# The first layer's modulation weights through a ring of four buffers instead of two

## The chip, the cores and the metric

The kernel runs on one core of one Trainium2 chip. The metric is the device time of one execution in microseconds (us). The kernel before takes 1497.33 us, the median of 3 runs (1495.65 to 1498.18). A difference of 0.2%, about 3.0 us, is what a measurement of this kernel can tell from no change.

## The reference

Two trunk layers are computed for 512 latent tokens and 128 context tokens that share one set of weights (model width 1024). Before each layer, six modulation vectors (shift, scale and gate, for the mixer and for the MLP) come from a conditioning vector:

```python
def ada_params(cond, w, b):
    m = jax.nn.silu(cond) @ w + b
    return jnp.split(m[..., None, :], 6, axis=-1)

def modulate(x, shift, scale):
    return layer_norm(x) * (1.0 + scale) + shift
```

There are two conditioning vectors, one for each kind of token, so `ada_params` is a product of 2 rows with a 1024 x 6144 matrix `ada_w[layer]`: nearly no arithmetic, but 24 MB of weights per layer. Layer 0's mixer is a pair of RG-LRU scans beside a 2-D Fourier mix, layer 1's is attention; after either comes a squared-ReLU MLP with 4096 hidden channels.

## The kernel before

**Weights.** All matmul weights come as units of 128 x 1024 floats (512 KB) in a fixed plan (`stream_plan`). `fetch` (L242) loads unit after unit into 3 `raw` buffers; `split_unit` splits each into a high half (ACT, L173) and a low half (DVE, L174) in one of 4 `sp` buffers. In names such as `raw_17` or `sp_14` the number is the unit's place in the plan. TensorE (PE) multiplies them in three passes (high x high, high x low, low x high). All matmuls but transposes are recorded at L265.

**The even mixer.** The plan begins with: units 1 to 4 (`in`, RNN input), 5 (`gate`), 6 to 9 (`four`), 10 (`gate`), 11 to 13 (`in`, gate chunks), 14 to 16 (`dft`), 17 (`in`), and from 18 the output projection `out`. Units 14 and 15 make the position DFT: 4 chunks of 12 matmuls, 48 in all, with 512 columns each. After it come the context DFT and the channel DFT (`yb_out`), the last gate chunk, and the output projection.

**Modulation weights of layer 0.** A third of them is used in `start`. The other two thirds (groups 1 and 2) are the work of `ada_gen`: a generator that is advanced once by each call of `next`, so once for each unit that PE takes. Each advance is a *step*: two loads of 512 KB (halves 0 and 1 of one block of 128 rows) and four matmuls on 32 columns of the array each (`ada_mm`), which add into one PSUM bank over 8 steps. In this text the steps are numbered 0 to 15; step 7 ends group 1 and step 15 ends group 2. `fill` keeps two loads outstanding: the load for step s+1 goes into the buffer that step s has just read. The buffers are two of the six `n` buffers (128 x 1024 floats each), the same two each time, since `last=True` takes back the buffer that was given back last:

```python
        def fill():
            nonlocal i
            while i < len(todo) and len(q) < 2:
                w = self.n.get([128, 1024], last=i >= 2)
                self.ada_load(*todo[i], w.t)
```

`acc` is one buffer of 128 x 2 x 1024 floats. It holds the sums of `ada_sum_gen`, which makes layer 1's modulation on DVE from the first layer's MLP on; until then nobody uses it.

**What sets the order.** A scheduler orders each engine's instructions when the kernel is built; each engine then runs its own list strictly in that order. Nearly all loads (L242, L381, L345, L337, L965) stand in one list, SP's: a load that has to wait for its buffer holds up all loads behind it.

Of the kernel before, what the change touches and what calls it, by code (L numbers as in the profile page):

```python
# [126 lines left out]
class Kern:  # L127
# [118 lines left out]
    def next(self, key):  # L246
        self.seen += 1
        self.ada_due += self.ada_rate
        while self.ada_due >= 1.0:
            self.ada_due -= 1.0  # L250
            if next(self.ada, None):
                break
        for _ in range(self.side_steps if self.side is not None else 0):
            next(self.side, None)
        assert self.plan[self.pos] == key, (self.plan[self.pos], key)
        self.pos += 1
        if not self.ready:
            self.pump()
        s = self.ready.pop(0)
        self.pump()  # L260
        return s
# [157 lines left out]
    def ada_gen(self, groups):  # L419

        todo = [(l, g, k, half) for l, g in groups for k in range(8) for half in range(2)]
        q = []
        i = 0

        def fill():
            nonlocal i
            while i < len(todo) and len(q) < 2:
                w = self.n.get([128, 1024], last=i >= 2)
                self.ada_load(*todo[i], w.t)
                q.append(w)  # L430
                i += 1
        fill()
        yield
        bank = fin = None
        for l, g, k, half in todo:
            if k == 0 and half == 0:
                bank = self.psum()
            w = q.pop(0)
            self.ada_mm(bank.t, k, half, w.t)
            w.done()  # L440
            fill()
            if k == 7 and half == 1:
                fin = self.ada_finish(l, g, bank)
                next(fin)
            if half == 1:
                yield
                if k == ADA_FIN and fin is not None:
                    next(fin, None)
                    fin = None
        if fin is not None:  # L450
            next(fin, None)

# [1290 lines left out]
```

## Time and profile before

| | before |
|---|---|
| median of 3 runs | 1497.33 us |
| the profiled execution | 1502.44 us |
| its span, first to last instruction | 1500.3 us |
| PE busy | 1443.6 us (96%) |
| DVE, ACT, POOL busy | 944.5, 618.9, 377.9 us |
| mean granted clock of PE, as a share of 2.4 GHz | 0.987 |

The profile is of one execution, 5.1 us above the median. Its traces show each engine's instructions, what ended the idle time before them, and the clock that PE was granted. Times within it count from the span's start.

### The profile page before, as it was taken

Reading aid. Unit: us, or ns where it says so; the run is one execution under the profiler, and the core shown is the slowest. Engines: PE = TensorE matmul, PEld = TensorE weight load, DVE = VectorE, ACT = ScalarE, POOL = GpSimd, SP = SyncE. Lnnn points to the kernel's source line nnn. Section 1 sums busy time; section 2 is a strip of 40 time slices with the busy share of each in tenths; the row PEclk is TensorE's granted clock in tenths of the full one; section 3 lists DMA queues with packets and bytes.
Section 4 is the critical chain, followed back from the end, with each engine's and each line's share of the span. In section 5 each row is a group of like instructions: output and inputs, shape, how many; then the busy total and the mean of one; then the engine's idle time right before and its main releaser. Section 6 shows DMA issues by size and latency. Waiting matters only on the chain. (4 is left out here: it accounts for less than half of the span.)

```text
span 1500.3 us, 21820 instructions
## 1 busy us (share of the span) xinstructions
PE 1443.6 (96%) x8428; PEld 1245.2 (83%) x8428; DVE 944.5 (63%) x1641; ACT 618.9 (41%) x1081; POOL 377.9 (25%) x395
## 2 busy tenths in 40 slices
PE   6999999999999999999799999999999999999997
PEld 4768677988988998998688888878898888998986
DVE  6656767857757663346645345556967893764865
ACT  4467437421321321335456355655631441431441
POOL 1144203202102202002413222321206633524510
PEclk9999999999999999999999999999999999999999
DMA  9354843445345342220633132330545434334441
GB/s 383 133 182 162 292 145 101 166 141 172 130 162 167 128 148 70 71 99 28 224 110 104 63 114 85 123 135 29 171 144 149 101 118 105 92 119 87 124 176 70
DMA packets 63575, 199.72 MB, mean 133 GB/s; under 512 B 11240, under 2 KB 11624, under 8 KB 63472
## 3 DMA queue, kind: packets, MB, share of 16 engines
q1 hardware_dynamic: 58320, 189.38, 36.5%
q0 software_dynamic: 5152, 8.95, 3.7%
q8 instruction: 66, 1.08, 0.3%
q14 instruction: 37, 0.30, 0.1%
HBM read 181.49 MB, written 16.81 MB: 132 GB/s over the span
## 5 line engine op out<-in xcount | busy, mean ns | idle before, releaser
L265 PE MATMUL bank<-R,sp 128*128 128x384 f32 (+3 forms) x4224 | 644.0, 311 | 13.5 <-POOL R L353 4.0
L265 PEld LDWEIGHTS bank<-R,sp 128*128 128x128 f32 x4224 | 620.9, 189 | 31.8 <-POOL R L353 5.8
L265 PE MATMUL bank<-sp,R 128*128 128x512 f32 x2580 | 614.2, 396 | 12.3 <-DVE sp L174 7.2
L265 PEld LDWEIGHTS bank<-sp,R 128*128 128x128 f32 x2580 | 484.2, 190 | 134.3 <-issue 10.3
L174 DVE TENSOR_TENSOR sp<-raw,sp 128x1024 fp32r<-128x1024 f32 (+2 forms) x177 | 235.8, 1334 | 132.6 <-ACT sp L173 130.8
L173 ACT ACTIVATE sp<-raw 128x1024 fp32r<-128x1024 f32 (+2 forms) x177 | 180.7, 1026 | 282.6 <-PE bank L265 254.6
L546 POOL TENSOR_TENSOR R<-R,n 128x512 f32<-128x512 f32 x30 | 45.5, 1557 | 278.0 <-DVE n L543 278.0
L354 DVE TENSOR_TENSOR R<-n,R 128x640 fp32r<-128x640 f32 (+2 forms) x119 | 106.5, 899 | 12.8 <-POOL R L353 9.7
L485 DVE SCALAR_TENSOR_TENSOR acc<-n,cx,acc 128x1024 f32<-128x1024 f32 x84 | 106.9, 1310 | 9.2 <-DMA n<-in_ada_w_dram 9.2
L1073 ACT ACTIVATE n<-bank,pack 128x384 f32<-128x384 f32 (+1 forms) x80 | 38.7, 525 | 138.5 <-PE bank L265 130.2
L351 ACT ACTIVATE R<-n 128x640 fp32r<-128x640 f32 (+1 forms) x96 | 66.9, 704 | 62.0 <-DVE n L1075 31.2
L567 POOL TENSOR_TENSOR ln<-ln,mhalf 128x1 f32<-128x1 f32 x35 | 22.4, 641 | 241.6 <-DVE ln L566 240.6
L565 ACT ACTIVATE junk<-R,ln 128x1024 bf16<-128x1024 f32 x35 | 40.3, 1150 | 86.1 <-DVE ln L575 60.8
L1075 DVE SCALAR_TENSOR_TENSOR n<-n 128x640 f32<-128x640 f32 x40 | 34.8, 871 | 64.3 <-ACT n L1073 64.2
L543 DVE TENSOR_TENSOR n<-bank,vec 128x512 f32<-128x512 f32 x70 | 47.3, 685 | 31.4 <-PE bank L265 29.3
L1423 POOL TENSOR_SCALAR n<-n,mx 128x384 f32<-128x384 f32 (+1 forms) x80 | 43.3, 544 | 90.6 <-DVE mx L1420 49.9
L265 PE MATMUL bank<-R,R 128*128 128x512 f32 x240 | 62.5, 405 | 0.0
L620 ACT ACTIVATE n<-bank,mod 128x128 f32<-128x128 f32 x120 | 45.4, 456 | 25.7 <-PE bank L613 25.7
L265 PEld LDWEIGHTS bank<-R,R 128*128 128x128 f32 x240 | 44.4, 188 | 11.0
L1437 ACT ACTIVATE n<-bank 128x384 f32<-128x384 f32 (+1 forms) x80 | 32.9, 447 | 49.4 <-PE bank L1433 43.0
L173 ACT ACTIVATE sp<-vec 128x1024 fp32r<-128x1024 f32 x24 | 25.3, 1058 | 57.7 <-PE bank L265 57.5
L1408 DVE CUSTOM_DVE_ANT_0 n<-bank,vec 128x256 f32<-128x256 f32 (+3 forms) x128 | 40.6, 350 | 12.9 <-PE bank L265 8.9
(179 smaller groups left out, 1246.9 us busy)
## 6 DMA issues: line engine op xcount, KB each, us to landing
raw<-in_wts_dram SPq DMA_DIRECT2D x184, 512.0 KB, 3.3
n<-in_ada_w_dram SPq DMA_DIRECT2D x80, 512.0 KB, 4.3
vec<-in_rpb_dram SPq DMA_DIRECT2D x16, 512.0 KB, 4.8
R<-in_ada_dram SPq DMA_DIRECT2D x15, 512.0 KB, 10.0
xsum<-n POOLq DMA_DIRECT2D x30, 256.0 KB, 5.6
vec<-in_vecs_dram SPq DMA_DIRECT2D x13, 512.0 KB, 4.6
vec<-gscr SPq DMA_DIRECT2D x10, 512.0 KB, 4.3
R<-in_x_dram SPq DMA_DIRECT2D x5, 512.0 KB
```

What stands on the lines that cost most here:

```text
L173: self.nc.scalar.activation(s.t[:, 0, :cols], src[:, :cols], AF.Copy)
L174: self.nc.vector.tensor_tensor(out=s.t[:, 1, :cols], in0=src[:, :cols], in1=s.t[:, 0, :cols].bitcast(F32), op=OP.subtract)
L265: self.nc.tensor.matmul(out, lhsT, rhs, start=start, stop=stop)
L351: self.nc.scalar.activation(hi, src, AF.Copy)
L354: (self.nc.vector if lo_eng == "dve" else self.nc.gpsimd).tensor_tensor(out=lo, in0=src, in1=hi.bitcast(F32), op=OP.subtract)
L485: nc.vector.scalar_tensor_tensor(acc.t[:, cond, :], w.t, f[cond], acc.t[:, cond, :], op0=OP.mult, op1=OP.add)
L543: nc.vector.tensor_tensor(out=tmp.t[:, :512], in0=o.t, in1=gates[t // 4].t[:, c], op=OP.mult)
L546: nc.gpsimd.tensor_tensor(out=x[:, t, c], in0=x[:, t, c], in1=tmp.t[:, :512], op=OP.add)
L565: nc.scalar.activation(self.junk, src, AF.Square, bias=m[:, 2:3], accum_out=m[:, 4:5])
L620: nc.scalar.activation(dst, tr.t[:, j * 128:(j + 1) * 128], AF.Identity, bias=sh, scale=sc)
L1408: nc.vector.tensor_tensor_reduce(out=p[h].t[:, c0:c1], in0=o[h].t[:, c0:c1], in1=rpb[j, h].t[:, r0:r0 + c1 - c0], scale=1.0, scalar=-3e38, ...
L1423: nc.gpsimd.tensor_scalar(p.t[:, :n], p.t[:, :n], m[:, 5:6], 1.0, op0=OP.mult, op1=OP.mult)
```

## The change

`ada_gen` takes two `n` buffers and the `acc` buffer at its start, holds them until its last step is done, and uses the four places in turn: steps with an even number use the two `n` buffers, steps with an odd number the two halves of `acc`. Four loads are outstanding instead of two.

```diff
     def ada_gen(self, groups):
 
         todo = [(l, g, k, half) for l, g in groups for k in range(8) for half in range(2)]
+        held = [self.n.get([128, 1024]) for _ in range(2)] + [self.acc.get([128, 2, 1024])]
+        bufs = [held[0].t, held[1].t, held[2].t[:, 0], held[2].t[:, 1]]
         q = []
         i = 0
 
         def fill():
             nonlocal i
-            while i < len(todo) and len(q) < 2:
-                w = self.n.get([128, 1024], last=i >= 2)
-                self.ada_load(*todo[i], w.t)
+            while i < len(todo) and len(q) < 4:
+                w = bufs[i % 4]
+                self.ada_load(*todo[i], w)
                 q.append(w)
                 i += 1
         fill()
...
             w = q.pop(0)
-            self.ada_mm(bank.t, k, half, w.t)
-            w.done()
+            self.ada_mm(bank.t, k, half, w)
             fill()
...
+        for w in held:
+            w.done()
         if fin is not None:
             next(fin, None)
```

The scheduler makes new lists from this. In the rows below, `in_ada_w_dram` marks a load of a step and `cx` a matmul of a step; the bank is the step's PSUM bank. Three places differ where the prediction speaks of them.

SP's list around the position DFT, before. `n_48`, `n_49` are step 9's loads, `n_50`, `n_51` step 10's, `n_52`, `n_53` step 11's; `vec` from `gscr` are the gates of group 1:

```order
L381 DMA n_48_1286<-in_ada_w_dram 128x1024
L381 DMA n_49_1290<-in_ada_w_dram 128x1024
L345 DMA vec_5_1750<-gscr 128x1024
L381 DMA n_50_1351<-in_ada_w_dram 128x1024
L381 DMA n_51_1355<-in_ada_w_dram 128x1024
L345 DMA vec_6_1752<-gscr 128x1024
L242 DMA raw_17_1295<-in_wts_dram 128x1024
L242 DMA raw_18_1360<-in_wts_dram 128x1024
L381 DMA n_52_1417<-in_ada_w_dram 128x1024
L381 DMA n_53_1421<-in_ada_w_dram 128x1024
L242 DMA raw_19_1426<-in_wts_dram 128x1024
```

The same place after the change. The pair in `n_11` and `n_12` is step 10's, the pair in `acc_1` behind it is step 11's, and the next pair is step 12's:

```order
L381 DMA n_11_559<-in_ada_w_dram 128x1024
L381 DMA n_12_560<-in_ada_w_dram 128x1024
L381 DMA acc_1_561<-in_ada_w_dram 128x1024 x2
L345 DMA vec_5_1725<-gscr 128x1024
L345 DMA vec_6_1727<-gscr 128x1024
L242 DMA raw_17_1280<-in_wts_dram 128x1024
L242 DMA raw_18_1343<-in_wts_dram 128x1024
L381 DMA n_11_559<-in_ada_w_dram 128x1024
L381 DMA n_12_560<-in_ada_w_dram 128x1024
L242 DMA raw_19_1407<-in_wts_dram 128x1024
```

Step 11's loads have moved ahead of both gate vectors and two weight units.

PE's list from step 10 into the position DFT, before:

```order
L265 MATMUL bank_67_1283<-n_51_1355,cx_118 32x512 x2
L410 MATMUL bank_72_1430<-ident,n_47_1223 128x128 x4
L265 MATMUL bank_73_1452<-sp_14_1292,R_11_877 128x512 x6
L265 MATMUL bank_73_1452<-sp_15_1357,R_11_877 128x512 x6
L265 MATMUL bank_74_1467<-sp_14_1292,R_11_877 128x512 x5
L265 MATMUL bank_67_1283<-n_52_1417,cx_118 32x512 x2
L265 MATMUL bank_74_1467<-sp_14_1292,R_11_877 128x512
L265 MATMUL bank_74_1467<-sp_15_1357,R_11_877 128x512 x2
L265 MATMUL bank_67_1283<-n_53_1421,cx_118 32x512 x2
L265 MATMUL bank_74_1467<-sp_15_1357,R_11_877 128x512 x4
```

and after the change:

```order
L265 MATMUL bank_67_1270<-n_12_560,cx_118 32x512 x2
L410 MATMUL bank_72_1411<-ident,n_31_1210 128x128 x4
L265 MATMUL bank_67_1270<-acc_1_561,cx_118 32x512 x4
L265 MATMUL bank_73_1431<-sp_14_1277,R_11_876 128x512 x6
L265 MATMUL bank_73_1431<-sp_15_1340,R_11_876 128x512 x6
L265 MATMUL bank_74_1446<-sp_14_1277,R_11_876 128x512 x6
L265 MATMUL bank_74_1446<-sp_15_1340,R_11_876 128x512 x6
```

Step 11 stands ahead of the DFT in one run of four matmuls; before, its two halves stood inside it.

PE's list around unit 8 (the third `four` unit), before. `n_28`, `n_29` are step 4, `n_30` and `n_31` step 5:

```order
L265 MATMUL bank_25_645<-n_28_928,cx_118 32x512 x2
L265 MATMUL bank_25_645<-n_29_932,cx_118 32x512 x2
L265 MATMUL bank_44_891<-sp_8_886,R_7_400 128x512
...
L265 MATMUL bank_48_919<-sp_8_886,R_7_400 128x512
L265 MATMUL bank_25_645<-n_30_971,cx_118 32x512 x2
L265 MATMUL bank_49_1089<-R_9_565,sp_10_977 128x384 x2
L265 MATMUL bank_50_1094<-R_9_565,sp_10_977 128x256 x2
L265 MATMUL bank_25_645<-n_31_975,cx_118 32x512 x2
L265 MATMUL bank_44_891<-sp_8_886,R_7_400 128x512 x5
```

and after the change, where the first two rows are the rest of step 4, the third is step 5, the next `n_11` and `n_12` are step 6, and the last `acc_1` is a lone first matmul of step 7:

```order
L265 MATMUL bank_25_648<-n_11_559,cx_118 32x512
L265 MATMUL bank_25_648<-n_12_560,cx_118 32x512 x2
L265 MATMUL bank_25_648<-acc_1_561,cx_118 32x512 x4
L265 MATMUL bank_44_888<-sp_8_883,R_7_400 128x512
...
L265 MATMUL bank_48_916<-sp_8_883,R_7_400 128x512
L265 MATMUL bank_25_648<-n_11_559,cx_118 32x512 x2
L265 MATMUL bank_49_1078<-R_9_568,sp_10_970 128x384 x2
L265 MATMUL bank_50_1083<-R_9_568,sp_10_970 128x256
L265 MATMUL bank_25_648<-n_12_560,cx_118 32x512 x2
L265 MATMUL bank_50_1083<-R_9_568,sp_10_970 128x256
L265 MATMUL bank_25_648<-acc_1_561,cx_118 32x512
L265 MATMUL bank_44_888<-sp_8_883,R_7_400 128x512 x5
```

One step and a lone matmul more have been reached here than before; between the two stretches on unit 8 stands one run more. Further on, steps 14 and 15 stand in one run of eight matmuls ahead of unit 18; before, step 14 was one run there and step 15 two runs inside unit 18's matmuls. Behind the output projection's first tiles all five lists are the same as before.

## Rows read from the trace of the kernel before

**Rows 1.** Page, part 1: busy time, share of the span and instructions, by engine.

```profile
PE 1443.6 (96%) x8428; PEld 1245.2 (83%) x8428; DVE 944.5 (63%) x1641; ACT 618.9 (41%) x1081; POOL 377.9 (25%) x395
```

**Rows 2.** Waits of PE from 30 to 215 us: total, times, longest (us).

```profile
PE bank L265 <- DMA n<-in_ada_w_dram: 5.6, 3, 3.1
```

**Rows 3.** PE's timeline, steps 4 to 6: start, us, line, operation, count [idle before <- releaser].

```profile
78.41 7.10 PE L265 MATMUL bank<-sp,R 128*128 128x512 f32 x30
...
93.46 1.06 PE L265 MATMUL bank<-n,cx 128*32 128x512 f32 x8
94.45 1.43 PE L265 MATMUL bank<-sp,R 128*128 128x512 f32 x5
98.25 1.05 PE L265 MATMUL bank<-n,cx 128*32 128x512 f32 x4 [2.36 <-DMA n<-in_ada_w_dram]
...
100.13 1.92 PE L265 MATMUL bank<-n,cx 128*32 128x512 f32 x4
102.79 14.64 PE L265 MATMUL bank<-sp,R 128*128 128x512 f32 x55 [0.74 <-DVE sp L174]
117.36 1.06 PE L265 MATMUL bank<-n,cx 128*32 128x512 f32 x8
```

**Rows 4.** PE's timeline, steps 10 to 15.

```profile
149.66 1.32 PE L265 MATMUL bank<-n,cx 128*32 128x512 f32 x8
...
151.33 4.14 PE L265 MATMUL bank<-sp,R 128*128 128x512 f32 x17
158.52 1.92 PE L265 MATMUL bank<-n,cx 128*32 128x512 f32 x4 [3.05 <-DMA n<-in_ada_w_dram]
...
170.80 1.06 PE L265 MATMUL bank<-n,cx 128*32 128x512 f32 x8
...
173.97 5.25 PE L265 MATMUL bank<-R,sp 128*128 128x66 f32 x44 [0.16 <-DVE R L354]
...
194.12 1.05 PE L265 MATMUL bank<-n,cx 128*32 128x512 f32 x4
...
195.99 1.05 PE L265 MATMUL bank<-n,cx 128*32 128x512 f32 x4
```

**Rows 5.** SP's timeline, loads: issue, us for issuing, line, load, count.

```profile
94.55 0.80 SPq L381 DMA_DIRECT2D n<-in_ada_w_dram  x2
...
142.97 0.86 SPq L381 DMA_DIRECT2D n<-in_ada_w_dram  x2
...
150.94 1.46 SPq L242 DMA_DIRECT2D raw<-in_wts_dram  x2
152.49 0.86 SPq L381 DMA_DIRECT2D n<-in_ada_w_dram  x2
```

**Rows 6.** Stretches: us, then busy (count) by engine, granted clock, DMA share, GB/s.

```profile
99.50:106.50 7.00, 6.26 (x17) 3.52 (x17) 6.86 (x6) 0.00 (x0) 4.90 (x4) 0.52 0.69 220
...
157.50:164.50 7.00, 5.98 (x13) 1.81 (x14) 3.79 (x7) 2.48 (x5) 0.00 (x0) 0.52 0.62 229
...
249.00:256.00 7.00, 4.35 (x21) 3.34 (x20) 6.89 (x16) 5.30 (x10) 2.39 (x4) 1.00 0.58 205
272.00:279.00 7.00, 5.14 (x43) 4.88 (x42) 7.00 (x9) 3.02 (x5) 0.51 (x1) 1.00 0.24 76
...
155.00:200.00 45.00, 41.78 (x224) 29.09 (x223) 32.29 (x67) 20.33 (x41) 5.83 (x4) 0.92 0.81 295
```

**Rows 7.** POOL's timeline: the first instruction that reads the gates of group 1.

```profile
178.06 2.38 POOL L557 TENSOR_TENSOR n<-vec,vec 128x1024 f32<-128x1024 f32 x1 [24.03 <-DVE R L354]
```

**Rows 8.** PE's timeline behind the even mixer: four waits under 2 us.

```profile
250.85 0.44 PE L265 MATMUL bank<-R,sp 128*128 128x384 f32 x1 [1.47 <-POOL R L353]
...
274.23 39.59 PE L265 MATMUL bank<-R,sp 128*128 128x256 f32 x287 [1.86 <-DVE R L354]
...
717.82 2.07 PE L265 MATMUL bank<-sp,R 128*128 128x512 f32 x7 [1.02 <-DVE sp L174]
...
721.59 6.66 PE L265 MATMUL bank<-sp,R 128*128 128x512 f32 x28 [1.70 <-DVE sp L174]
```

## The prediction

> **What bounds the kernel now.** I read the page's busy times first: PE is busy 96% of the span, the next engine 63% [rows 1]. So time is to be had only where PE stands still or runs slowly, in the stretch that the change touches. The list of PE's waits from 30 to 215 us names what it waited for: loads of modulation weights, 5.6 us in 3 waits, the longest 3.1 us [rows 2]. PE's own timeline shows the two that matter: 2.36 us ahead of step 5 [rows 3] and 3.05 us ahead of step 11 [rows 4]. The view of stretches shows what followed either: 7.0 us with a mean granted clock of 0.52, so nearly all at 1.2 GHz [rows 6]. While the clock is down, a half step costs 1.92 us [rows 3] instead of 1.05 [rows 4]. A stall here costs its wait and the slow stretch behind it.
>
> SP's timeline shows why the loads came late. With two buffers a step's loads can be issued only when the step before has been multiplied. Step 5's pair went out at 94.55 us [rows 5], when step 4, begun at 93.46, had ended; PE wanted it five matmuls later and got it at 98.25 [rows 3], 3.7 us after the issue. Step 11's pair had to wait for step 10 (149.66 to 150.98 [rows 4]), stood behind two weight units issued at 150.94, went out at 152.49 [rows 5], and was there at 158.52 [rows 4], 6.0 us after.
>
> **The change, part by part.** It adds no instruction: the same 32 loads and 64 matmuls, other buffers. `acc` lies idle until the first MLP, after all 16 steps; the two held `n` buffers were the ring's before too. These edits cost nothing.
>
> *Step 11.* Its loads now wait for step 9 and not for step 10. Step 9's end released the pair issued at 142.97 [rows 5]; the new list has step 11's pair there, ahead of the gate vectors and the weight units. With either delay seen, 3.7 or 6.0 us, it lands at 147 to 149, and PE comes to it at about 151: no wait, no slow clock. The gate vector `vec_5`, which this pair is moved past, goes out under 1 us later; its reader starts at 178.06 [rows 7], so that is covered. Before, the 48 DFT matmuls and step 11 took from 151.33 to 170.80 [rows 4], 19.47 us. Thirty such matmuls take 7.10 us at the whole clock [rows 3], so 48 take 11.36, and step 11 as one run takes 1.06, as step 12 does [rows 4]: 12.42. The term is **-7.05 us**.
>
> *Steps 4 to 7.* Here the wait stays. I take the end of unit 7 as before, 93.46 us. The rest of step 4 and the whole of step 5 now follow in one run, about 2 us instead of 1, then the five matmuls of unit 8 (1.43 us [rows 3]): PE is ready for step 6 at about 96.9. Step 6's load needs step 4's buffer, so it still goes out near 94.55 and lands near 98.25. The wait shrinks from 2.36 to about 1.4 us, but PE goes on at the same time as before. It then has one run more (the lone matmul of step 7) before it comes back to unit 8, whose low half DVE delivers at 102.79 as before, for DVE's list up to there is unchanged: PE waited 0.74 us for it [rows 3], so it was ready at 102.05. If the clock falls as before, the extra run costs about 1.9 us: ready at 103.95, 1.16 later than 102.79. Behind that, steps 6 and 7 were two runs and the rest of step 7 is one: -1.06 us (the row at 117.36 [rows 3]). Together **+0.1 us**. The bounds: if the clock does not fall, the extra run fits ahead of 102.79, and the stretch from 102.79 to 106.5 at half clock (3.7 us) gives back 1.85: -1.85 - 1.06 = -2.9. If it falls only at 102.8 and stays down 7.0 us, half of 7.0 is lost instead of half of 3.7: +1.65 - 1.06 = +0.6; both bad sides give +1.2. The trace has no wait of 1.4 us amid 32-column runs. I take the fall, since it is the nearest: here the clock was down from 99.5 on, behind a wait at the same place.
>
> *Steps 14 and 15.* Before, three runs: step 14 like step 12, 1.06, and the halves of step 15, 1.05 each [rows 4], 3.16 us in all. A half step costs as much as a whole one, so it is rounds that cost, not matmuls. Eight matmuls in one run do not occur before. They could take one round (1.06) or as much as three (3.16); there are four places of 32 columns, so I take two, 2.12: **-1.04 us**, bounds -2.1 and 0. Of this the skill has a rule: the Trainium skill's page TensorEngine Tiling (Array Packing), under Key Properties, says that a change of tiling mode drains the engine. By it each run kept whole saves one drain into and one out of the 32-column mode, so the term would be larger than mine, for which no row gives a price of its own; the equal price of half and whole runs would then hold the drain.
>
> *Behind step 11* everything comes about 7 us earlier. The channel DFT waits 0.16 us for DVE [rows 4], so DVE is close there; but from 155 to 200 us it is busy 32.29 of 45 us [rows 6], and its work follows PE's DFT chunks, so it moves along. I add nothing.
>
> The sum is -7.05 + 0.1 - 1.04 = **-8.0 us**. Against the profiled execution's 1502.44 us that gives 1494.4; the median of the runs lies 5.1 us below the profiled time, and taken from 1497.33 the forecast is **1489.3 us**.
>
> **Rivals.**
>
> (a) *The first fall goes too.* For it: the wait ahead of step 6 is only 1.4 us, and PE waited 1.47 and 1.86 us elsewhere [rows 8] with the clock whole through both stretches [rows 6]. Against: here 32-column runs and a second wait, for unit 8's low half, follow at once. It gives -7.05 - 2.9 - 1.04 = -11.0: 1486.3 us.
>
> (b) *DMA takes back half.* From 155 to 200 us the DMA engines are busy 0.81 of 45 us [rows 6], 36.5 us. In 8 us less they would be busy nearly throughout, even with step 11's pair gone to an earlier place. If weight units for the output projection then land late, PE waits there, and about 4 us of the 8 are left: 1493.3. Against: the longest delay seen here is the 6.0 us above, and the units keep their order.
>
> (c) *Nothing changes.* Behind the DFT comes DVE's work on its result, and PE already waits 0.16 us for it [rows 4]. If DVE and not PE sets the end of the even mixer, PE's gain turns into waits for DVE there. Time: 1497.3. Against: DVE's 32.29 of 45 us [rows 6] leave it 12.7 us, more than the 8. A rule points the same way: the Trainium skill, Trainium Kernel Development and Optimization, under Best Practices, asks for double buffering to overlap transfers with compute; the ring of two has that already, and by this rule alone the sum would be 0. The trace agrees for most steps (outside the two stalls only 0.2 of the 5.6 us are left [rows 2 to 4]) and disagrees at step 11, by 3.05 us.
>
> (d) *Slower, by the clock.* All that follows comes about 8 us earlier and may meet the clock's control at another moment. If the waits of 1.47 and 1.86 us and the pair of 1.02 and 1.70 us [rows 8] are each followed by 7.0 us at half clock, as the two stalls here were [rows 6], the first two cost 3.5 each, and the pair, 3.8 us apart, holds the clock down for 10.8 and costs 5.4: 12.4 - 8.0 = +4.4, so 1501.7 us. It decides when two of the three have fallen and the third falls too. Against: the clock stayed whole through the first two [rows 6].
>
> **How the numbers follow.** My forecast has 0.50, (a) 0.20, (b) 0.13, (c) 0.12, (d) 0.05. A measurement of this kernel can tell 0.2%, 3.0 us, from no change. The forecast, (a) and (b) are faster by more: 0.83; (c) is the same: 0.12; (d) is slower: 0.05. The forecast's own range, with the bounds of steps 4 to 7 and 14 to 15, is 1485 to 1491.5; (a) with them begins at 1485.3, (b) is at 1493.3. I take 1485.0 to 1495.0, which leaves out (c), (d) and a little of the rest.
>
> **What would show it right or wrong.** Right: in PE's waits of the even mixer the loads of modulation weights fall from 5.6 us to about 1.5, all of it ahead of step 6; no wait in the DFT, its 48 matmuls in 11.4 us at clock 1.00; one 7 us stretch at half clock instead of two near 100 to 170 us; span near 1492. Rival (a): no such stretch. Rival (b): waits of PE for DVE's or ACT's splits from units 18 to 25 on. Rival (c): PE waits for DVE's split of units 14 or 15. Rival (d): clock below 1.00 near 240 to 280 us. My step on steps 4 to 7 is wrong if PE does not wait ahead of step 6, the one on 14 and 15 if their run takes much other than 2.1 us.

## The result and the profile after

The changed kernel takes 1488.01 us (median of 4 runs, 1487.56 to 1489.6) where the kernel before takes 1497.44 us beside it (4 runs, 1495.65 to 1498.18): a ratio of 0.9933, with an interval of 0.992 to 0.9946, or 9.4 us less. A second set of runs gave 1491.25 against 1500.44 us, 0.9938 (0.9922 to 0.9954). The profiled execution of the changed kernel took 1488.42 us, its span 1486.6. The experiments below ran beside a kernel before of 1499.84 or 1500.44 us, so they are compared by their ratio to it, and an interval is always that of the ratio. One of the seven executions of the kernel "loads two ahead in the text" took 4956 us where the other six took 1491 to 1496; no ratio here counts it.

The busy times of the page, which answer to [rows 1]: PE is busy for 10.4 us less with the same number of instructions, so the same instructions run faster; none was taken out.

```profile
PE 1433.2 (96%) x8428; PEld 1241.7 (84%) x8428; DVE 941.4 (63%) x1641; ACT 619.1 (42%) x1081; POOL 375.9 (25%) x395
```

PE's waits from 30 to 215 us, after (total, times, longest), to be held against [rows 2]: the loads of modulation weights fell from 5.6 us to 2.5. Of these, 1.62 us stand ahead of step 6 and 0.83 ahead of the first matmul of step 4. A wait of 1.2 us ahead of the transposes at L410 is new.

```profile
PE bank L265 <- DMA n<-in_ada_w_dram: 2.5, 2, 1.6
PE bank L410 <- DVE n L395: 1.2, 1, 1.2
PE bank L265 <- DVE sp L174: 0.9, 1, 0.9
```

PE's timeline after, steps 4 to 8 (start, us, line, operation, count, [idle before <- releaser]), against [rows 3]:

```profile
76.87 1.05 PE L265 MATMUL bank<-n,cx 128*32 128x512 f32 x2 [0.83 <-DMA n<-in_ada_w_dram]
...
92.16 1.44 PE L265 MATMUL bank<-acc,cx 128*32 128x512 f32 x7
93.53 1.44 PE L265 MATMUL bank<-sp,R 128*128 128x512 f32 x5
96.60 1.05 PE L265 MATMUL bank<-n,cx 128*32 128x512 f32 x4 [1.62 <-DMA n<-in_ada_w_dram]
98.24 1.05 PE L265 MATMUL bank<-n,cx 128*32 128x512 f32 x4
99.54 1.05 PE L265 MATMUL bank<-acc,cx 128*32 128x512 f32 x2
101.52 12.87 PE L265 MATMUL bank<-sp,R 128*128 128x512 f32 x55 [0.94 <-DVE sp L174]
116.85 1.06 PE L265 MATMUL bank<-acc,cx 128*32 128x512 f32 x6
128.90 1.06 PE L265 MATMUL bank<-n,cx 128*32 128x512 f32 x8
```

Steps 4 and 5 are one run, step 6 waits 1.62 us, the lone first matmul of step 7 (two rows, `x2`, where a step has eight) stands ahead of unit 8's rest, and that rest waits 0.94 us for DVE's split, as before. But it takes 12.87 us where it took 14.64 [rows 3]: the clock is whole.

PE's timeline after, steps 10 to 15 and the first wait of [rows 8], against [rows 4]:

```profile
145.43 1.06 PE L265 MATMUL bank<-n,cx 128*32 128x512 f32 x8
...
147.02 1.06 PE L265 MATMUL bank<-acc,cx 128*32 128x512 f32 x8
148.01 11.27 PE L265 MATMUL bank<-sp,R 128*128 128x512 f32 x48
159.21 1.07 PE L265 MATMUL bank<-n,cx 128*32 128x512 f32 x8
...
175.84 1.06 PE L265 MATMUL bank<-n,cx 128*32 128x512 f32 x8
176.72 1.04 PE L265 MATMUL bank<-acc,cx 128*32 128x512 f32 x8
177.69 6.23 PE L265 MATMUL bank<-sp,R 128*128 128x512 f32 x26
185.16 0.66 PE L410 MATMUL bank<-ident,n 128*128 128x128 f32 x4 [1.23 <-DVE n L395]
...
239.22 0.44 PE L265 MATMUL bank<-R,sp 128*128 128x384 f32 x1 [1.45 <-POOL R L353]
```

Step 11 starts without a wait and the 48 DFT matmuls run through in 11.27 us. Its loads stand in SP's timeline after ahead of the gate vectors and the weight units, where [rows 5] had them last:

```profile
138.26 0.80 SPq L381 DMA_DIRECT2D acc<-in_ada_w_dram  x2
139.79 6.15 SPq L345 DMA_DIRECT2D vec<-gscr  x2
148.19 1.47 SPq L242 DMA_DIRECT2D raw<-in_wts_dram  x2
```

The stretches after (as in [rows 6]: busy times, granted clock, DMA share, GB/s) show the clock at 1.00 in both places, so both stretches at 1.2 GHz are gone in this execution:

```profile
95.00:107.00 12.00, 9.46 (x38) 5.61 (x39) 11.23 (x10) 1.06 (x1) 8.16 (x5) 1.00 0.81 299
150.00:168.00 18.00, 17.83 (x113) 14.65 (x115) 16.61 (x43) 11.39 (x25) 2.81 (x3) 1.00 0.96 373
```

To compare executions, whose starts differ by a microsecond or two, I cut PE's timeline at four rows: the last 128x256 run on `n` in `start` (47.22 before, 45.95 after, below), step 8, step 12, and the wait of 1.45 us for POOL of [rows 8]. Part A lies between the first two, B (with steps 10 and 11 and the DFT) between the next, C (with steps 14 and 15) between the last. From PE's timeline before, the two rows that are not among those shown:

```profile
47.22 0.64 PE L265 MATMUL bank<-n,cx 128*32 128x256 f32 x8
...
133.12 1.07 PE L265 MATMUL bank<-n,cx 128*32 128x512 f32 x8
```

and after:

```profile
45.95 0.64 PE L265 MATMUL bank<-n,cx 128*32 128x256 f32 x8
```

In the table each line is one profiled execution; a kernel with two lines was profiled twice.

| kernel (profile) | A, us | B, us | C, us | half clock in A and B, us |
|---|---|---|---|---|
| before | 85.90 | 37.68 | 80.05 | 6.7 and 6.8 |
| before, second profile | 84.62 | 36.88 | 80.09 | 3.4 and 3.2 |
| after | 82.95 | 30.31 | 80.01 | 0 and 0 |
| after, second profile | 82.99 | 30.93 | 80.18 | 0 and 0 |
| four places from step 8 on | 84.56 | 30.32 | 79.83 | 3.4 and 0 |
| the same, second profile | 84.20 | 30.31 | 79.97 | 3.4 and 0 |
| four places up to step 7 | 84.45 | 38.55 | 80.03 | 3.4 and 6.8 |
| the same, second profile | 82.96 | 38.67 | 80.07 | 0 and 6.8 |
| loads two ahead in the text | 82.97 | 30.31 | 81.75 | 0 and 0 |
| three places | 86.80 | 32.68 | 79.74 | 0 and 0 |
| five places | 82.58 | 31.61 | 80.81 | 0 and 0 |
| step 6 loaded late | 85.98 | 30.31 | 80.05 | 6.7 and 0 |
| the same, second profile | 85.96 | 30.31 | 79.89 | 6.7 and 0 |
| bias loaded early | 83.47 | 30.33 | 80.20 | 0 and 0 |

The last column is worked out from the stretches 95 to 107 and 150 to 168 us of each run: twice the part of the clock that is missing, times the width (0.72 over 12 us: 2 x 0.28 x 12 = 6.7). It counts all time at half clock, also time in which PE stands.

Between the first profiles A is 2.95 us shorter, B 7.37, C 0.04: 10.36 us. Between the second ones it is 1.63, 5.95 and, in C, 0.09 longer: 7.49. The timed 9.4 and 9.2 us lie between. Ahead of the first cut and behind the last the executions scatter too: the first pair of spans differs by 13.7 us, of which 2.1 lie behind the last cut, while in the second pair the changed kernel takes 1.5 us more there. So a single pair of profiles says what happens at a place, and the timed runs say what the change is worth.

### The profile page after: what moved, and what is told of

It is laid out like the page before. It is cut to its first block, busy times and chain, and to the rows that moved or that the text cites. A ratio compares the mean times of both kernels' runs of the same rounds, so it can differ in the third digit from the quotient of the medians.

```text
span 1486.6 us, 21822 instructions
## 1 busy us (share of the span) xinstructions
PE 1433.2 (96%) x8428; PEld 1241.7 (84%) x8428; DVE 941.4 (63%) x1641; ACT 619.1 (42%) x1081; POOL 375.9 (25%) x395
## 5 line engine op out<-in xcount | busy, mean ns | idle before, releaser
L265 PE MATMUL bank<-sp,R 128*128 128x512 f32 x2580 | 608.1, 394 | 11.4 <-DVE sp L174 6.1
```

The source lines that it names most:

```text
L265: self.nc.tensor.matmul(out, lhsT, rhs, start=start, stop=stop)
```

## The experiments

**Half of the ring each.** Both kernels give a load its place by number, and let it go out once that place has been read.

```diff
+        place = lambda i: i % 4 if i >= 16 else i % 2
...
-            while i < len(todo) and len(q) < 4:
-                w = bufs[i % 4]
+            while i < len(todo) and len(q) < 4 and place(i) not in [p for p, _ in q]:
+                w = bufs[place(i)]
...
```

> Four places from step 8 on, the ring of two before it. My theory (two separate stalls, each a wait for a late load and a stretch at half clock behind it): PE stands for about 2.4 us ahead of step 5 as before, 6 to 7 us at half clock follow near 100, and step 8 starts as far behind unit 8's start as before; step 11 runs whole ahead of the DFT, whose 48 matmuls take 11.3 us at clock 1.00 (19.47 us become 12.4, -7.05); steps 14 and 15 run as one (-1.04, with a wait of about 1.2 us ahead of the transposes taken back as in the changed kernel). Sum -7 to -8: 1489.5 to 1490.5 us. Rival 1, the half clock near 100 came by the moment and not by the wait: no such stretch here either, 1487 to 1488. Rival 2, all of the gain hangs on the first stretch: 1495 or more.

The other kernel has `i < 16` in the same line.

> Four places up to step 7, the ring of two from step 8 on. My theory: waits of about 1.6 and 0.9 us ahead of step 6 and of unit 8's low half, no half clock near 100, step 8 about 2.9 us earlier behind unit 7 than before; the wait of about 3 us ahead of step 11 amid the DFT and 7 us at a clock of 0.52 behind it stay, so does step 15 in two runs. Sum -2.9: 1494 to 1495 us. Rival 1, the half clock comes by the moment and not by the wait: the DFT, reached 3 us earlier, waits but runs on at 1.00, 1490.5. Rival 2, the first stretch is bound by DVE's split and gives nothing: 1497.

With four places from step 8 on: 1492.78 us against 1499.84 before, 0.9956 (0.9941 to 0.9971), -6.6 us. Its PE timeline has the wait ahead of step 5 and none in the DFT; the stretch view has half clock in the first place alone, 3.4 us of it where I had expected 6 to 7:

```profile
97.46 1.69 PE L265 MATMUL bank<-n,cx 128*32 128x512 f32 x4 [2.47 <-DMA n<-in_ada_w_dram]
...
148.46 1.06 PE L265 MATMUL bank<-acc,cx 128*32 128x512 f32 x8
149.46 11.27 PE L265 MATMUL bank<-sp,R 128*128 128x512 f32 x48
```

```profile
95.00:107.00 12.00, 9.54 (x35) 5.79 (x36) 9.95 (x9) 0.00 (x0) 7.99 (x5) 0.86 0.68 233
150.00:168.00 18.00, 17.70 (x106) 14.54 (x105) 15.39 (x36) 11.52 (x25) 1.42 (x2) 1.00 0.98 360
```

With four places up to step 7: 1496.97 us, 0.9982 (0.9971 to 0.9993), -2.7 us. Its PE timeline and stretches show the reverse, but not quite: a wait of 1.97 us, and 3.4 us at half clock behind it, where I had expected none. (This profile is of the slowest of the kernel's 12 executions, 1503.09 us.)

```profile
99.64 1.05 PE L265 MATMUL bank<-n,cx 128*32 128x512 f32 x4 [1.97 <-DMA n<-in_ada_w_dram]
...
104.01 1.13 PE L265 MATMUL bank<-acc,cx 128*32 128x512 f32 x2
...
159.34 1.92 PE L265 MATMUL bank<-n,cx 128*32 128x512 f32 x4 [3.10 <-DMA n<-in_ada_w_dram]
```

```profile
95.00:107.00 12.00, 10.03 (x40) 4.09 (x31) 12.00 (x12) 1.76 (x2) 8.27 (x6) 0.86 0.78 269
150.00:168.00 18.00, 14.19 (x52) 8.04 (x49) 11.86 (x21) 5.01 (x10) 4.21 (x4) 0.81 0.73 237
```

So the gain has two parts that can be had apart, and within their intervals (4.3 to 8.8 us and 1.0 to 4.3) they add up: 6.6 + 2.7 = 9.3. The larger part, some 6.6 of the 9.4 us, comes from step 8 on, where step 11 is. Rival 2 of the first kernel, all of it from the first stretch, is out; so is rival 2 of the second, nothing from it. Rival 1 of either is out too: the clock fell behind both waits that came back.

**Buffers or program text.**

```diff
-            while i < len(todo) and len(q) < 4:
+            while i < len(todo) and len(q) < 2 and place(i) not in [p for p, _ in q]:
...
```

with `place = lambda i: i % 4`.

> Four places in turn, but the program text issues a step's loads only two half steps ahead, as before the change. My theory: only the buffer that a load must wait for counts, since the scheduler places the loads by when their buffer is free; the waits and clocks are those of the changed kernel, 1487.5 to 1489. Rival, the gain comes from being four loads ahead in the text: the waits ahead of steps 5 and 11 are back, 1495 to 1497.

1493.05 us, 0.9956 (0.9939 to 0.9972). Parts A and B are those of the changed kernel to 0.02 us, with no half clock: where a load stands in the text does not matter there, only when its place is free. It matters in part C, 1.7 us longer: step 15's loads go out 3.9 us later behind step 12 than in the changed kernel (172.46 - 159.13 against 168.67 - 159.21), half of the step waits for its load, and the run of eight falls apart again, as PE's timeline shows.

```profile
180.85 1.05 PE L265 MATMUL bank<-acc,cx 128*32 128x512 f32 x4 [0.86 <-DMA acc<-in_ada_w_dram]
...
182.98 1.05 PE L265 MATMUL bank<-acc,cx 128*32 128x512 f32 x4
```

Both of the expectations were too simple: the four loads in the text do nothing for the two stalls and keep steps 14 and 15 together.

**Three places, five places.** The one has `i % 3`, two `n` buffers and one half of `acc`, and three loads outstanding; the other holds a third `n` buffer and has `i % 5` and five loads outstanding. The edit of the five:

```diff
-        held = [self.n.get([128, 1024]) for _ in range(2)] + [self.acc.get([128, 2, 1024])]
-        bufs = [held[0].t, held[1].t, held[2].t[:, 0], held[2].t[:, 1]]
+        held = [self.n.get([128, 1024]) for _ in range(3)] + [self.acc.get([128, 2, 1024])]
+        bufs = [held[0].t, held[1].t, held[2].t, held[3].t[:, 0], held[3].t[:, 1]]
...
```

> Three places (two n buffers and one half of acc), three loads ahead. Half a step of step 11 then still needs the buffer of step 10's first half and stands amid the DFT, behind 16 of its matmuls; its other half runs ahead of the DFT. My theory, a load needs about 3.7 to 6 us from the moment its buffer is free: that half waits 0.5 to 3 us; with a wait over 2.4 us half clock follows and the time is 1492 to 1495, with a shorter one the clock stays whole and the time is 1489 to 1491. Rival, a third buffer does all: no wait in the DFT, 1488.

> Five places, three of them n buffers. My theory: step 6's wait for its buffer goes (1.6 us less ahead of step 6), but PE then waits longer for unit 8's low half, which DVE delivers when it did, so nothing is gained there: within 1.5 us of the changed kernel. Rival 1, loads still bound the changed kernel ahead of step 6: 1.5 us or more faster. Rival 2, a third n buffer held all through the even mixer makes other users of the six n buffers wait: slower by 2 us or more.

Three: 1495.9 us against 1499.84, 0.997 (0.9959 to 0.9982), -4.5 us by the ratio. PE's timeline has the half of step 11 amid the DFT with a wait of 1.16 us and the clock whole, as my theory had it; B is 2.4 us above the changed kernel's. But the time is some 2 us above what I expected (0.997 of 1497.3 is 1492.8, and I had said 1489 to 1491), since part A grew to 86.80 us, 3.85 more than in the changed kernel. Its rows show twelve runs of 32-column matmuls in place of ten, about 1 us each, and a new wait of 1.22 us for DVE (L908); why DVE is late there I have not followed up.

```profile
151.26 1.05 PE L265 MATMUL bank<-n,cx 128*32 128x512 f32 x4
...
157.34 1.05 PE L265 MATMUL bank<-acc,cx 128*32 128x512 f32 x4 [1.16 <-DMA acc<-in_ada_w_dram]
```

Five: 1494.22 us against 1500.44, 0.9948 (0.9932 to 0.9965). The interval overlaps the changed kernel's, so a gain is not shown, and whether it is slower stays open. Its sum of A, B and C is 195.00 us, the changed kernel's second profile 194.10. A wait for a load is still there, 2.00 us for part of step 6, against my theory:

```profile
97.56 1.05 PE L265 MATMUL bank<-acc,cx 128*32 128x512 f32 x2 [2.00 <-DMA acc<-in_ada_w_dram]
...
102.34 12.87 PE L265 MATMUL bank<-sp,R 128*128 128x512 f32 x55 [0.81 <-DVE sp L174]
```

But unit 8's rest begins 55.56 us behind the first cut (46.78), as with two places and with four (55.57). It begins when DVE's split is there, so a fifth place has nothing to give at this point.

**One long wait in the place of two short ones.** Step 6's loads are issued twice into the same places; the order then puts step 6 behind units 8 and 9.

```diff
-                self.ada_load(*todo[i], w)
+                for _ in range(2 if i in (12, 13) else 1):
+                    self.ada_load(*todo[i], w)
```

> The changed kernel with step 6's two loads issued twice into the same halves: the pair lands later, and the order puts step 6 behind units 8 and 9, so PE stands in one piece from about 97 to 101.5 us, some 4 us, where it stood for 1.6 and 0.9 with work between. The 1.06 us of step 6 move behind the wait. My theory, a wait of over 2.4 us is followed by half clock: 3.4 to 7 us of it, which cost 1.7 to 3.5: 2.8 to 4.5 us slower than the changed kernel. Rival, the half clock comes by the moment or by the short 32-column runs and not by the length of the wait: clock 1.00, about 1.1 us slower than the changed kernel.

1494.17 us against the changed kernel's 1491.25 and 1500.44 before: 0.9967 (0.9951 to 0.9982), so 2.9 us of the gain are lost (4.4 by the ratios). PE's timeline and the stretch view:

```profile
102.20 14.70 PE L265 MATMUL bank<-sp,R 128*128 128x512 f32 x55 [5.39 <-DVE sp L174]
```

```profile
95.00:107.00 12.00, 6.61 (x22) 5.20 (x22) 10.77 (x10) 0.34 (x1) 8.39 (x5) 0.72 0.88 299
```

Unit 8's rest begins where it began, 55.58 us behind the first cut (55.57 in the changed kernel), but takes 14.70 us as before the change, and A is 85.98 us. The half clock costs 1.83 us here (14.70 - 12.87), and step 6, moved behind the wait, the other 1.2 of the 3.0 us that A has grown by. The short runs of steps 6 and 7 between the waits thus do two things: they use time in which PE stands anyway, and they part one wait of 5.4 us into shorter ones, behind which the clock stayed whole in five of six profiles.

**The new wait.** Each group's bias is loaded at its fifth step instead of behind its last.

```diff
...
+            if k == 4 and half == 0:
+                ab = self.ada_bias(l, g)
...
-                fin = self.ada_finish(l, g, bank)
+                fin = self.ada_finish(l, g, bank, ab)
```

> The changed kernel with each group's bias loaded four steps earlier. In the changed kernel the last group's bias is issued at 172.87 and holds DVE's sum at line 395 up by 0.51 us, and PE waits 1.23 us for that sum ahead of the last transposes. My theory, the late bias takes 0.5 us of the run of eight back, and DVE's list, which has this sum behind a gated sum at 182.68, the rest: the wait falls from 1.2 to about 0.7, the time by 0.5 us (0.0003, less than a measurement can tell). Rival 1, the order changes with the load, DVE sums earlier and the whole 1.2 us go. Rival 2, the longer held n buffer makes other loads wait: over 1 us slower.

1490.91 us, 0.9933 (0.9915 to 0.9951): no different from the changed kernel, 1491.25 beside it. PE's wait did not shrink, it is 1.43 us, and so it was in the changed kernel's second profile. DVE's timeline, first after, then with the early bias:

```profile
182.68 1.22 DVE L562 SCALAR_TENSOR_TENSOR R<-R,n 128x1024 f32<-128x1024 f32 x1
184.41 0.69 DVE L395 TENSOR_TENSOR n<-bank,n 128x512 f32<-128x512 f32 x1 [0.51 <-DMA n<-in_ada_b_dram]
```

```profile
186.06 1.21 DVE L567 SCALAR_TENSOR_TENSOR R<-R,n 128x1024 f32<-128x1024 f32 x1
187.20 0.68 DVE L398 TENSOR_TENSOR n<-bank,n 128x512 f32<-128x512 f32 x1
```

The wait for the bias (0.51 us, 0.87 in the changed kernel's second profile) is gone, and the sum starts as soon as the gated sum ahead of it on DVE is done. But in this execution that gated sum itself begins later: 24.26 us behind step 12 (161.80) against 23.47 in the changed kernel, so PE waits as long as before. All three of my cases fall. In the changed kernel the load came last, here DVE's list did; that the load alone sets the wait is out, and what an early bias would give if DVE's list did not move stays open.

**The same kernels again.** 

> The changed kernel once more, beside the runs that follow and with a second profile. My theory: 0.9933 of the time before (0.992 to 0.995); no wait in the DFT, waits of about 1.6 and 0.9 us ahead of unit 8's low half. Since waits of 1.97, 2.36, 2.47 and 3.1 us were followed by half clock in the runs so far, and waits of 1.62, 1.75 and 2.01 were not, I expect no half clock near 100. Rival, half clock behind these waits comes in some executions and not in others: 3.4 us of it here or a wider spread of the times.

1491.25 us, with no half clock near 100 behind waits of 1.75 and 1.55 us.

> A second look at the kernel before. If the length of a wait sets the half clock, the waits of 2.36 and 3.05 us come again and behind each 7 us at half clock. If the moment has a part in it, one of the two stretches is shorter (3.4 us, as behind the waits of 2.47 and 1.97 us in two runs) or not there, with the same waits.

> A second look at the kernel with four places up to step 7. Near 100 us its waits of 1.97 us and no second one were followed by 3.4 us at half clock; the wait of 3.1 us in the DFT by 7. If the length of a wait decides, the same again. If the moment has a part, the first stretch is 0 or 7 us here; the wait of 3.1 is followed by 3.4 or 7.

> A second look at the kernel with four places from step 8 on, whose wait of 2.47 us was followed by 3.4 us at half clock where the kernel before had 2.36 us and 7.0. If the length of a wait decides, 3.4 us again; if the moment has a part, 0 or 7 us.

> A second look at the kernel with one wait of 5.4 us ahead of unit 8's low half. My theory: half clock behind it again, 7 us of it (never none, since the wait is over 3 us). If the moment alone decides, none or 3.4 us.

One execution each: 1496.05, 1497.07, 1492.46 and 1494.29 us, with 1498.1 of the kernel before beside them. PE's timeline and the stretches of the kernel before, second profile:

```profile
98.22 1.35 PE L265 MATMUL bank<-n,cx 128*32 128x512 f32 x4 [2.23 <-DMA n<-in_ada_w_dram]
...
156.94 1.92 PE L265 MATMUL bank<-n,cx 128*32 128x512 f32 x4 [3.03 <-DMA n<-in_ada_w_dram]
```

```profile
95.00:107.00 12.00, 9.77 (x37) 5.63 (x36) 10.63 (x10) 0.18 (x1) 8.42 (x5) 0.86 0.66 220
150.00:168.00 18.00, 14.97 (x60) 9.22 (x60) 11.06 (x20) 7.52 (x14) 2.58 (x2) 0.91 0.82 280
```

The waits are those of [rows 3] and [rows 4] within 0.13 us, and both stretches at half clock are half as long: 3.4 and 3.2 us. So the length of a wait alone does not decide; the moment, or something else that differs between executions, has a part. The length seems to have one too: the two profiles with waits of 5.4 and 5.5 us both show 6.7 us, those with 2.47 and 2.45 both 3.4, and the four places up to step 7 show none in the second profile, whose wait was 1.64 instead of 1.97 us. What decides between 3.4 and 6.7 us at the same wait stays open.

A shorter wait shows the same at another place. The wait for POOL at the last cut is 1.45 to 1.54 us long in all 14 profiles. In ten of them the clock stays whole behind it; in four (the second profiles of the kernel before, of the changed kernel and of four places from step 8 on, and the five places) some 3.4 us at half clock follow. From the second profile of the changed kernel:

```profile
241.44 0.44 PE L265 MATMUL bank<-R,sp 128*128 128x384 f32 x1 [1.46 <-POOL R L353]
```

```profile
240.00:290.00 50.00, 46.47 (x305) 44.95 (x306) 43.12 (x54) 27.37 (x51) 12.95 (x11) 0.97 0.56 182
```

## Why the prediction was right, and where it was not

The forecast was 1489.3 us, the time is 1488.01. That closeness is in part luck: two errors in the terms, of opposite sign, are part of it. The time lies between the forecast and rival (a)'s 1486.3, and of the two signs near 100 us it was rival (a)'s that came, no stretch at half clock.

**What bounds the kernel** held. The two stalls and the slow stretches behind them were the time to be had: each half of the ring that was given back brought its stall back with it.

**Step 11**, -7.05 us: right. Its loads went out where the order had them, PE did not wait, and from its first row to step 12 it took 147.02 to 159.21, 12.19 us, where the prediction had 12.42. Part B fell by 7.37 us. The size hangs on the execution, though: between the second profiles it is 5.95, for the half clock in the kernel before lasted 3.2 us there and not 6.8. I took the price of a slow stretch from one execution, which had two long ones and lay 5.1 us above the median.

**Steps 4 to 7**, +0.1 us: the geometry was right, the choice between its two cases wrong. PE waited 1.62 us for step 6 (1.4 predicted; not all of the waits for loads stood there, since step 4's first matmul waited 0.83), and unit 8's rest began 55.57 us behind the first cut before and after. The step that failed is "I take the fall, since it is the nearest". Six profiles have this order here (the changed kernel twice, the loads two ahead, the early bias, and the four places up to step 7 twice). In five the clock stayed whole, behind waits of 1.62 to 1.82 us; in the sixth it fell for 3.4 us, behind 1.97. The term came out at its lower bound: -2.95 us in the first pair of profiles, against -2.9, and -1.63 in the second. That is rival (a)'s mechanism, to which I gave 0.20. The waits of 1.47 and 1.86 us of [rows 8], followed by a whole clock, turned out the nearer rows, and not the wait of 2.36 at the same place. But they were no safe ground either, since the wait of 1.47 us is the one at the last cut, which half clock followed in four of the 14 profiles. Of the bounds, the +1.2 for "both bad sides" does not add up: the two give 1.16 + 1.65 - 1.06 = +1.75, and they exclude each other, since in one the clock falls before 102.8 and in the other only then.

**Steps 14 and 15**, -1.04 us: the run was mis-sized only a little, 1.85 us from its start to the next row (175.84 to 177.69) against 2.12. What the term left out is what is late next. PE comes to the transposes sooner, and DVE's sum at L395 does not: the new wait of 1.23 us. Part C shows it, 80.05 us before and 80.01 after. Nothing of the term is left: PE waits for DVE, by the mechanism that rival (c) named for another place.

**Behind step 11** nothing more was won or lost: C is the same within 0.17 us in the four profiles of the two kernels.

**The rivals.** (b) fell: in the changed kernel PE waits for no load between 155 and 215 us, and DVE's and ACT's splits hold nobody up there. (c) fell but for the 1.2 us: PE does not wait for units 14 or 15 in the first profile and 0.35 us in the second. The number of places tells the same: three take 4.5 us less than two, four take 9.2 less. The Trainium skill (Trainium Kernel Development and Optimization, under Best Practices) asks for double buffering to overlap transfers with compute. Read as "two are enough", it would give no gain for three or for four; the runs disagree. (d) did not decide: the second profile of the changed kernel had some 3 us at half clock between 240 and 290 us (0.97 of 50 us), but so had the kernel before in its second profile, so it comes and goes with the execution and not with the change.

In sum, from the first pair of profiles: -7.37 - 2.95 - 0.04 = -10.4 where the prediction had -8.0; timed, -9.4.

## What to carry to other kernels

When a transfer waits for its buffer, count from the moment that the buffer comes free to the moment that PE wants the data: two buffers overlap transfer and compute only if that distance exceeds the transfer's delay, and here it did not, by more than 2 us, at 2 of 16 steps. Take the price of a slow clock from more than one execution, and look for short work that can stand inside an unavoidable wait, since it also keeps PE from standing in one long piece (one wait of 5.4 us brought 6.7 us at half clock in both its profiles). For every run that is made shorter, read off which other engine has to deliver next, or the gain ends in a new wait as it did at the transposes.

## What the runs showed of the hardware that I had not expected

The same list of instructions with the same waits (2.36 and 2.23 us, 3.05 and 3.03 us) is followed by 6.7 us at 1.2 GHz in one execution and by 3.4 or less in another; no other length but 0 was seen in these two places. Ahead of unit 8, waits of up to 1.82 us amid 32-column runs left the clock whole in all five profiles; one of 1.97 us did not, and 2.00 and 2.01 us (five and three places) did. At another place a wait of only 1.45 to 1.54 us was followed by half clock in four profiles of 14, so a short wait is no warrant for a whole clock.

A run of eight matmuls on 32 columns that the trace counts as 16 rows takes 1.85 us from its start to the next row (175.84 to 177.69), one of four 0.99 (147.02 to 148.01), and the lone matmul of step 7 is 1.05 us long where a whole step is 1.06: the price goes by rounds of up to four, so a lone half step costs as much as a whole one [rows 4].
